# New places for the steps of an attention head within its period of 40 ticks, and per-column places for the split of the next weights

## The chip, the cores and the metric

The kernel runs on one core of a Trainium2 chip. The metric is the device time of one execution in microseconds (us). The engines that compute are TensorE (PE, matmuls), VectorE (DVE), ScalarE (ACT) and GpSimd (POOL); SyncE (SP) issues most of the DMAs. Each engine works through its own list of instructions strictly in order, and waits for the others by semaphores.

## The reference

One streaming inference step of one layer: 512 frames of a new stream (the prompt) and 64 frames of a running stream (the sample, which has 512 cached keys and values), 2048 channels each, in float32.

```python
def stick_breaking(q, k, v, q_pos, k_pos):
    z = jnp.einsum('bqhd,bkhd->bhqk', q, k) / math.sqrt(HEAD_DIM)
    mask = (k_pos[None, :] < q_pos[:, None])[None, None]
    log_1mb = jnp.where(mask, jax.nn.log_sigmoid(-z), 0.0)
    after = lax.cumsum(log_1mb, axis=3, reverse=True) - log_1mb
    w = jnp.where(mask, jnp.exp(jax.nn.log_sigmoid(z) + after), 0.0)
    return jnp.einsum('bhqk,bkhd->bqhd', w, v)

def hybrid_layer(x, ...):
    hn = rmsnorm(x, g_norm1)
    q, k, v, gb, gc, hc = split(hn @ w_in)       # 3 x 8 heads x 128, 3 x 1024 channels
    q = rmsnorm(q, g_q); k = rmsnorm(k, g_k)     # per head
    o_attn = stick_breaking_blocks(q, k, v, P)   # per head, causal; sample against cache and itself
    o_conv = gb * conv3(gc * hc)
    x = x + concat(rmsnorm(o_attn), rmsnorm(o_conv)) @ w_out
    h2 = rmsnorm(x, g_norm2)
    return x + (silu(h2 @ w_gate) * (h2 @ w_up)) @ w_down, k, v, new_conv
```

Keys and values of the new frames are outputs too.

## The kernel before

Frames lie along the free axis (576 = 512 + 64, in two halves of 288), channels on the 128 partitions. A float32 product is made of three matmuls on parts rounded to a shorter format: high x high, low x high, high x low. So each weight block is split into a high part (`whi`, a cast on ACT) and a low part (`wlo`, a subtraction on DVE), and so is everything else that is multiplied.

The kernel runs in stages: the input and the first four columns of 128 outputs of `w_in` (EARLY); units of a fast matrix scheme for other columns; then the stage of this document, from about 184 us on: ten columns of `w_in` (LATE: q and k of heads 4 to 7, v of heads 6 and 7), and after them six columns of the first convolution groups, while the eight attention heads are computed between their matmuls; then the convolution, the output projection and the feed-forward part, to the end at 2356 us.

In the stage of the heads `project` makes one column: `next_weight` hands over the split weights, then `product` runs over 16 blocks of 128 channels for each half of the frames, three matmuls a block (`step`, line 246). After each block comes `pipe.tick()`. A `Pipeline` holds generators with due times counted in these ticks; at a tick it runs those that are due, and what they emit goes to the end of each engine's list. A column is 32 ticks. So the ticks count places in the program: PE's order, and through `manual_schedule` that of ACT, DVE, POOL and SP too, is written out by hand in this stage, and a step's number says behind which matmuls and which other steps its instructions stand. It does not say when they run. In a tick, the generator that was put back first goes first.

Head h is the generator `attend(h)`, spawned at tick 1 + 40 h (`PERIOD`). It sorts the steps of `head_steps(h)` by their numbers, 0 to 127, and emits them. Three heads are under way at a time: while head h does its steps 0 to 39, head h - 1 does 40 to 79 and head h - 2 does 80 to 119. For the last head the numbers over 72 are squeezed to three quarters. In the order of the data, the steps of a head are:

- `load` (SP) brings q and k as 576 tokens; `square` (ACT) and `sums` (DVE) make their sums; `small` (PE, DVE, ACT), `root` (DVE) the scales; `norm` and `turn` (DVE) scale and transpose; `high` (ACT: `qh`, `qe`, `kh`, `ke`) and `low` (DVE) split them. `weigh` (POOL) and `keys` (SP, eight stores) put the new keys out. For heads 0 and 1, DVE also transposes in `square`.
- `cached` (SP) and `turn_cached` (DVE) bring the cached keys; `sample` (PE, then `zc` copied by ACT) makes the scores of the sample.
- For the prompt there are three groups of keys, b = 2 (which holds the blocks 2 and 3), 1 and 0, each with its PSUM bank `z2`, `z1`, `z0`: `score` (PE, then three activations), `add` (DVE, then the mask on POOL), `cast` (ACT), `rest` (DVE, then for b = 2 and 1 a sum on POOL), `sum_high` (ACT) and `sum_low` (DVE) of the sums, `run` (PE, DVE, an exponential and a cast on ACT), `run_low` (DVE).
- `values` (SP), `store` (SP), `v_high` (ACT: `vh`), `v_low` (DVE: `vl`); `out` and `outs` (PE) multiply values into the PSUM tile `po`; `copy` (ACT, line 1024) takes `po` out into `o_attn`, whose tiles are `o_oa` and `o_ob`.
- For the sample: `soft` (ACT), `soft_add` (DVE, five operations on POOL), `sp_high` (ACT: `sph`), `sp_low` (DVE), `sample_sums` (PE into the PSUM tile `cz`, line 1031, then DVE), `weights` (ACT), `load_cv` (SP), `sample_out` (PE `os`, ACT).
- `squares` (ACT, then POOL adds into `acc_a`), at the end of a head. Squares and the sums of `square` share one scratch area.

The PSUM tag `misc` has two buffers, taken in turn by `ss` (`small`), `zs` (`sample`), `po`, `cz` and `os`; in the order of emission `cz` takes the buffer that `po` had. Tiles of `t1` have one buffer each, apart from `vtok` with two.

Beside the heads, each LATE column i spawns `split_later(i, end)`: at its tick 7 both halves of the next weights' high part on ACT, at 9 and 11 their low parts on DVE, at 16 the load of the weights after the next on SP into the one raw buffer. When a half is done, `late_evac` transposes it out of PSUM (DVE `El`) and POOL issues its store to `qk_dram`.

```python
    def split_later(i, end):
        yield 7
        if i + 1 < end:
            yield from split_parts()
        yield 5
        if i >= len(EARLY) and i + 2 < end:
            load_weight()
```

Of the kernel before, what the change touches and what calls it, by code (L numbers as in the profile page):

```python
# [24 lines left out]
NH = 8  # L25
# [17 lines left out]
LATE = [(0, 4), (1, 4), (0, 5), (1, 5), (0, 6), (1, 6), (0, 7), (1, 7), (2, 6), (2, 7)]  # L43
PERIOD = 40


# [52 lines left out]
def tile_hybrid_stream_step(  # L99
# [100 lines left out]
    def split_parts():  # L200
# [567 lines left out]
    def head_steps(h):  # L768
# [31 lines left out]
        for i, n in enumerate("qk"):  # L800

            @at((0, 5)[i])
            def _(i=i, n=n):
                E[n] = t1.tile([P, T], F32, tag="E" + n, name="E" + n)
                nc.sync.dma_start(out=E[n], in_=qk_dram[2 * h + i])

            @at((12, 20)[i])
            def _(i=i, n=n):
                if (i, h) in EARLY:
                    nc.vector.transpose(out=E[n], in_=E[n])  # L810
                nc.scalar.activation(out=sq, in_=E[n], func=AF.Square)

            @at((14, 22)[i])
# [3 lines left out]
        @at(28)  # L817
# [6 lines left out]
        @at(31)  # L824
# [8 lines left out]
        @at(33)  # L833
        def _():
            stt(out=t_, in0=y, scalar=-0.5, in1=y, op0=ALU.mult, op1=ALU.mult)
            nc.vector.tensor_tensor(out=t_, in0=t_, in1=ms, op=ALU.mult)
            stt(out=ms, in0=t_, scalar=1.5, in1=y, op0=ALU.add, op1=ALU.mult)

        for i, n in enumerate("qk"):
            gain = (gqs, col("gk"))[i]  # L840

            @at((33, 35)[i])
            def _(i=i, n=n):
                r = ms[:, NB * i : NB * (i + 1)].unsqueeze(2).to_broadcast([P, NB, 32])
                nc.vector.tensor_tensor(out=chunks(E[n]), in0=chunks(E[n]), in1=r, op=ALU.mult)

            @at((35, 36)[i])
            def _(n=n):
                nc.vector.transpose(out=new(n + "f", T), in_=E[n])

            @at((37, 39)[i])
            def _(n=n, gain=gain):
                f = w[n + "f"]
                nc.scalar.activation(out=new(n + "h", cut[n], F32R), in_=f[:, : cut[n]], func=AF.Copy, scale=gain)
                nc.scalar.activation(out=new(n + "e", T - 3 * P), in_=f[:, 3 * P :], func=AF.Copy, scale=gain)

            @at((39, 41)[i])
            def _(n=n, gain=gain):
                stt(out=new(n + "l", TP, F32R)[:, : cut[n]] if n == "q" else new(n + "l", cut[n], F32R),
                    in0=w[n + "f"][:, : cut[n]], scalar=gain, in1=w[n + "h"].bitcast(F32), op0=ALU.mult,  # L860
                    op1=ALU.subtract)

        @at(42)
# [4 lines left out]
        @at(46)  # L868
# [4 lines left out]
        @at(47)  # L873
        def _():
            nc.vector.transpose(out=w["cK"], in_=w["cK"])
# [8 lines left out]

        for b, t in ((2, 52), (1, 56), (0, 61)):
# [9 lines left out]
        for b, t in ((2, 56), (1, 59), (0, 67)):  # L895

            @at(t)
# [5 lines left out]
        for b, t in ((2, 58), (1, 63), (0, 71)):  # L903

            @at(t)
            def _(b=b):
                cast(new(f"ph{b}", full[b], F32R), w[f"pr{b}"])

        for b, t in ((2, 60), (1, 65), (0, 75)):

            @at(t)
            def _(b=b):
                low(new(f"pl{b}", full[b], F32R), w[f"pr{b}"], w[f"ph{b}"])
                if b:
                    nc.gpsimd.tensor_tensor(out=pb(b)[:, P:], in0=pb(b)[:, P:], in1=pb(b + 1), op=ALU.add)

        for b, t0, t1_ in ((1, 65, 67), (0, 69, 71)):

            @at(t0)
            def _(b=b):  # L920
                cast(new(f"s{b}h", full[b + 1] if b == 0 else 256, F32R), pb(b + 1))

            @at(t1_)
# [3 lines left out]
        @at(62)  # L927
# [7 lines left out]
        @at(66)  # L935
        def _():
            load_values(h)

        @at(80)
        def _():  # L940
            soft_log(sp[:, :320], zc)

        @at(82)
# [8 lines left out]
        @at(72)  # L952
# [5 lines left out]
        @at(83)  # L958
        def _():
# [13 lines left out]

        for b, t in ((2, 78), (1, 81), (0, 86)):

            @at(t)
            def _(b=b):
# [5 lines left out]

        for b, t in ((2, 82), (1, 85), (0, 90)):

            @at(t)
# [4 lines left out]
        @at(83)  # L991
# [4 lines left out]
        @at(84)  # L996
# [4 lines left out]
        @at(90)  # L1001
        def _():
            w["po"] = misc("po")
            mm(w["po"][:, 384:512], w["vtok"][:, 3, :], pb(3), start=True, stop=False, skip_group_check=True)

        for i, t in ((2, 95), (1, 98), (0, 101)):

            @at(t)
            def _(i=i):
# [3 lines left out]

        @at(92)
        def _():
            cast(new("sph", T, F32R), sp)

        @at(94)
        def _():
            low(new("spl", T, F32R), sp, w["sph"])  # L1020

        @at(102)
        def _():
# [3 lines left out]

        @at(108)
        def _():
# [7 lines left out]

        @at(110)
        def _():
            nc.scalar.activation(out=w["ws"][:, TS:], in_=w["ws"][:, TS:], func=AF.Exp)  # L1040

        @at(118)
        def _():
# [6 lines left out]
        for i, (a, b) in enumerate(HALVES):  # L1050

            @at((119 if h == NH - 1 else 125) + 2 * i)
            def _(i=i, a=a, b=b):
# [1291 lines left out]
```

## Time and profile before

| what | us |
|---|---|
| median of 3 runs (lowest, highest) | 2358.49 (2356.91, 2360.97) |
| the profiled execution's own time | 2358.04 |
| its span, first to last instruction | 2356.3 |
| busy in the span: PE / DVE / ACT / POOL | 2326.7 / 1916.2 / 1164.5 / 280.3 |
| PE busy in the 20 us from 240, 340, 380 | 16.87, 16.10, 15.85 |
| PE busy in the 20 us from 440 and 460 | 20.00, 20.00 |

The profile is one execution. A group's row gives busy time and mean duration; a row of the waits tells which engine stood idle, before which instruction, until which other instruction ended, in total, how often, and the longest. In a timeline the bracket at the end of a row is the idle time before it and what ended it. Names such as `cz L1031` are tile and line of the kernel. PE's times are those of pipelined matmuls, which overlap: durations of neighbours must not be added, distances of their starts may be.

### The profile page before, as it was taken

Reading aid. Unit: us, or ns where it says so; the run is one execution under the profiler, and the core shown is the slowest. Engines: PE = TensorE matmul, PEld = TensorE weight load, DVE = VectorE, ACT = ScalarE, POOL = GpSimd, SP = SyncE. Lnnn points to the kernel's source line nnn. Section 1 sums busy time; section 2 is a strip of 40 time slices with the busy share of each in tenths; the row PEclk is TensorE's granted clock in tenths of the full one; section 3 lists DMA queues with packets and bytes.
Section 4 is the critical chain, followed back from the end, with each engine's and each line's share of the span. In section 5 each row is a group of like instructions: output and inputs, shape, how many; then the busy total and the mean of one; then the engine's idle time right before and its main releaser. Section 6 shows DMA issues by size and latency. Waiting matters only on the chain.

```text
span 2356.3 us, 43717 instructions
## 1 busy us (share of the span) xinstructions
PE 2326.7 (99%) x17437; PEld 2315.5 (98%) x17437; DVE 1916.2 (81%) x2846; ACT 1164.5 (49%) x2021; POOL 280.3 (12%) x394
## 2 busy tenths in 40 slices
PE   9999988999999999999999999999999999999999
PEld 9999888999999999999999999999999999999999
DVE  7976767688887889888888888888888777887886
ACT  7534766544445555444444444444444444444444
POOL 1002333121111220000000000000000001431121
PEclk9999999999999999999999999999999999999999
DMA  8775454784368645444444444444444945885643
GB/s 274 206 208 160 121 138 107 232 284 124 110 227 233 190 159 159 141 153 137 138 153 128 147 151 130 147 146 134 149 141 140 342 137 191 234 234 187 206 130 104
DMA packets 584869, 402.54 MB, mean 171 GB/s; under 512 B 91870, under 2 KB 571864, under 8 KB 584664
## 3 DMA queue, kind: packets, MB, share of 16 engines
q1 hardware_dynamic: 574136, 378.56, 51.5%
q0 software_dynamic: 10160, 20.94, 3.9%
q8 instruction: 136, 2.23, 0.4%
q14 instruction: 69, 0.57, 0.1%
q10 hardware_dynamic: 368, 0.24, 0.0%
HBM read 303.53 MB, written 96.16 MB: 170 GB/s over the span
## 4 chain that ended last, share of the span: by engine, by line
PE 87%; DVE 4%; ACT 3%; DMA 2%; issue 1%; POOL 1%; SPq 0%; DVEq 0%; ACTq 0%; POOLq 0%
PE psy L1991 35%; PE psw L1991 18%; PE psx L1991 9%; PE psy L1478 6%; PE pjo L246 4%; PE pj L246 4%; PE psw L1478 3%; PE psy L1125 3%; PE psx L1478 2%; PE psw L1125 1%; PE psx L1125 1%; ACT whi L205 1%; DVE wlo L208 0%; DMA vtok<-vt_dram 0%; DMA form_dram<-hf 0%
## 5 line engine op out<-in xcount | busy, mean ns | idle before, releaser
L1991 PE MATMUL psy<-h_s,whl 128*128 128x288 f32 x2787 | 411.4, 294 | 0.0
L1991 PEld LDWEIGHTS psy<-h_s,whl 128*128 128x128 f32 x2787 | 383.6, 188 | 0.0
L256 DVE TENSOR_TENSOR whl<-raw_a,whl 128x1024 fp32r<-128x1024 f32 (+4 forms) x296 | 319.2, 1080 | 57.3 <-ACT whl L255 56.4
L1991 PE MATMUL psw<-t,whl 128*128 128x288 f32 x2400 | 347.5, 295 | 0.0
L1991 PEld LDWEIGHTS psw<-t,whl 128*128 128x128 f32 x2400 | 327.6, 188 | 0.3 <-DVE whl L256 0.2
L255 ACT CAST whl<-raw_a 128x1024 fp32r<-128x1024 f32 (+4 forms) x296 | 268.1, 906 | 102.1 <-issue 35.3
L246 PE MATMUL pj<-x,whi 128*128 128x288 f32 x1248 | 275.4, 302 | 0.3 <-DVE x L409 0.3
L256 DVE TENSOR_TENSOR whl<-raw_b,whl 128x1024 fp32r<-128x1024 f32 (+5 forms) x190 | 199.3, 1049 | 66.2 <-ACT whl L255 65.2
L255 ACT CAST whl<-raw_b 128x1024 fp32r<-128x1024 f32 (+5 forms) x190 | 165.4, 871 | 166.1 <-issue 73.2
L2001 ACT COPY part<-psy 128x288 f32<-128x288 f32 x242 | 96.4, 398 | 282.6 <-PE psy L1991 281.4
L246 PEld LDWEIGHTS pj<-x,whi 128*128 128x128 f32 x1248 | 210.3, 191 | 1.1 <-DVE x L409 0.6
L246 PE MATMUL pj<-x,wlo 128*128 128x288 f32 x624 | 186.1, 298 | 0.1
L1991 PE MATMUL psy<-t2t,whl 128*128 128x288 f32 x1212 | 183.4, 295 | 0.0
L1991 PE MATMUL psy<-b22m,whl 128*128 128x288 f32 x1212 | 183.0, 294 | 0.0
L1991 PE MATMUL psx<-h_s,whl 128*128 128x288 f32 x1185 | 173.7, 295 | 0.0
L1991 PEld LDWEIGHTS psy<-t2t,whl 128*128 128x128 f32 x1212 | 168.4, 188 | 0.2 <-DVE whl L256 0.2
L1991 PEld LDWEIGHTS psy<-b22m,whl 128*128 128x128 f32 x1212 | 168.2, 188 | 0.0
L1991 PEld LDWEIGHTS psx<-h_s,whl 128*128 128x128 f32 x1185 | 162.7, 188 | 0.0
L255 ACT CAST whl<-s 128x1024 fp32r<-128x1024 f32 (+5 forms) x81 | 72.3, 893 | 101.3 <-PE psw L1991 101.3
L246 PEld LDWEIGHTS pj<-x,wlo 128*128 128x128 f32 x624 | 119.2, 191 | 0.7 <-DVE wlo L494 0.3
L1770 POOL DMA_DIRECT2D hid_dram<-form x3 | 2.3, 752 | 971.5 <-DVE form L256 970.2
L1991 PE MATMUL psy<-t,whl 128*128 128x288 f32 x576 | 106.7, 295 | 0.0
(533 smaller groups left out, 4546.6 us busy)
## 6 DMA issues: line engine op xcount, KB each, us to landing
hid_dram<-form SPq DMA_DIRECT2D x147, 288.0 KB, 2.2
raw_a<-in_w_in_dram SPq DMA_DIRECT2D x31, 1024.0 KB, 5.4
raw_a<-in_w_gate_dram SPq DMA_DIRECT2D x22, 1024.0 KB, 5.5
raw_a<-in_w_up_dram SPq DMA_DIRECT2D x22, 1024.0 KB, 5.7
raw_b<-in_w_gate_dram SPq DMA_DIRECT2D x22, 1024.0 KB, 6.8
raw_b<-in_w_up_dram SPq DMA_DIRECT2D x22, 1024.0 KB, 6.5
h_s<-hid_dram SPq DMA_DIRECT2D x10, 2016.0 KB, 11.8
raw_a<-in_w_out_dram SPq DMA_DIRECT2D x16, 1024.0 KB, 5.5
```

The source lines that it names most:

```text
L205: nc.scalar.copy(out=hi[:, a : a + 1024], in_=raw[:, a : a + 1024])
L246: mm(ps, w_[:, k, csl], x_, start=(k == 0 and n == 0), stop=(k == nk - 1 and n == 2))
L255: nc.scalar.copy(out=hi, in_=src)
L256: (lo_eng or nc.vector).tensor_tensor(out=lo, in0=src, in1=hi.bitcast(F32), op=ALU.subtract)
L1125: mm(ps, whl[:, w_, j, :], x_, start=(start and j == 0 and q == 0), stop=(j == NP - 1 and q == 2), skip_group_check=True)
L1478: mm(ps, whl[:, w_, j, :], x_, start=(start and j == 0 and q == 0), stop=(j == m - 1 and q == 2), skip_group_check=True)
L1770: q.dma_start(out=hid_dram[fp][2 * n - 2 : 2 * n].rearrange("f p t -> p f t"), in_=t.bitcast(F32))
L1991: mm(ps, whl[:, w_, j, :], x_, start=(start and j == 0 and q == 0), stop=(j == len(xs_) - 1 and q == 2), skip_group_check=True)
L2001: nc.scalar.copy(out=t, in_=st["y"])
```

## The change

Every number of a step moves into a table `STEP`; many get another value. For the ten LATE columns `split_later` hands over to a new function, `split_at`, which places the two casts, the two subtractions and the load by a table `WEIGHT` with one row of five ticks a column, the halves one by one. The instructions are the same; what changes is the order in which they are emitted on each engine. Tuples of `STEP` are for (q, k), for b = (0, 1, 2), or for the two halves.

| step | before | after | step | before | after |
|---|---|---|---|---|---|
| load q, k | 0, 5 | 0, 11 | values | 66 | 62 |
| square | 12, 20 | 13, 19 | store | 72 | 74 |
| sums | 14, 22 | 17, 21 | soft, soft_add | 80, 82 | 78, 83 |
| small, root | 31, 33 | 27, 30 | load_cv | 83 | 80 |
| norm q, k | 33, 35 | 35, 33 | run 0, 1, 2 | 86, 81, 78 | 86, 81, 72 |
| low q, k | 39, 41 | 40, 41 | run_low 0, 1, 2 | 90, 85, 82 | 89, 87, 86 |
| keys | 46 | 47 | v_high, v_low | 83, 84 | 75, 83 |
| score 0, 1, 2 | 61, 56, 52 | 61, 56, 50 | out | 90 | 87 |
| add 0, 1, 2 | 67, 59, 56 | 63, 62, 55 | outs 0, 1, 2 | 101, 98, 95 | 101, 97, 95 |
| cast 0, 1, 2 | 71, 63, 58 | 69, 63, 58 | sp_high, sp_low | 92, 94 | 92, 100 |
| rest 0, 1, 2 | 75, 65, 60 | 77, 65, 62 | sample_sums, weights | 108, 110 | 104, 109 |
| sum_high 0, 1 | 69, 65 | 67, 65 | sample_out | 118 | 116 |
| sum_low 0, 1 | 71, 67 | 77, 67 | squares | 125, 127 | 124, 125 |
| sample | 62 | 59 | squares, last head | 119, 121 | 119, 121 |

`cached` (28), `turn` (35, 36), `high` (37, 39), `weigh` (42), `turn_cached` (47) and `copy` (102) keep theirs.

```diff
+STEP = dict(
+    load=(0, 11), square=(13, 19), sums=(17, 21), cached=28, small=27, root=30, norm=(35, 33), turn=(35, 36),
...
+WEIGHT = [
+    (9, 11, 9, 14, 18), (11, 16, 11, 14, 24), (10, 12, 10, 17, 20), (7, 9, 7, 12, 12), (6, 11, 7, 10, 21), (6,
+    10, 7, 11, 19), (6, 9, 7, 11, 19), (7, 10, 7, 11, 16), (9, 11, 9, 17, 18), (5, 8, 6, 11, 16)]
...
+    def split_at(i, end):
+        w = {}
+
+        def begin():
+            w["raw"], w["two"] = raws[i + 1], weight_split(i + 1)
+
+        def high(a):
+            nc.scalar.copy(out=w["two"][0][:, a : a + 1024], in_=w["raw"][:, a : a + 1024])
+
+        def rest(a):
+            nc.vector.tensor_tensor(out=w["two"][1][:, a : a + 1024], in0=w["raw"][:, a : a + 1024],
+                                    in1=w["two"][0][:, a : a + 1024].bitcast(F32), op=ALU.subtract)
+
+        h0, l0, h1, l1, again = WEIGHT[i - len(EARLY)]
+        now = 0
+        steps = [(h0, begin), (h0, lambda: high(0)), (h1, lambda: high(1024)), (l0, lambda: rest(0)),
+                 (l1, lambda: rest(1024))] + [(again, load_weight)] * (i + 2 < end)
+        for t, work in sorted(steps, key=lambda step: step[0]):
+            if t > now:
+                yield t - now
+                now = t
+            work()
+
     def split_later(i, end):
+        if len(EARLY) <= i < len(EARLY) + len(LATE):
+            yield from split_at(i, end)
+            return
         yield 7
...
-            @at((0, 5)[i])
+            @at(STEP["load"][i])
...
-        for b, t in ((2, 78), (1, 81), (0, 86)):
-
-            @at(t)
+        for b in (2, 1, 0):
+
+            @at(STEP["run"][b])
...
-        @at(108)
+        @at(STEP["sample_sums"])
```

More of the change, by code (lines that the diff above doesn't have):

```diff
@@ L44 @@
 PERIOD = 40
+STEP = dict(
+    load=(0, 11), square=(13, 19), sums=(17, 21), cached=28, small=27, root=30, norm=(35, 33), turn=(35, 36),
+    high=(37, 39), low=(40, 41), weigh=42, keys=47, turn_cached=47, score=(61, 56, 50), add=(63, 62, 55),
+    cast=(69, 63, 58), rest=(77, 65, 62), sum_high=(67, 65), sum_low=(77, 67), sample=59, values=62, store=74,
+    soft=78, soft_add=83, load_cv=80, run=(86, 81, 72), run_low=(89, 87, 86), v_high=75, v_low=83, out=87,
+    outs=(101, 97, 95), sp_high=92, sp_low=100, copy=102, sample_sums=104, weights=109, sample_out=116,
+    squares=(124, 125), last=(119, 121))
+WEIGHT = [
+    (9, 11, 9, 14, 18), (11, 16, 11, 14, 24), (10, 12, 10, 17, 20), (7, 9, 7, 12, 12), (6, 11, 7, 10, 21), (6,
+    10, 7, 11, 19), (6, 9, 7, 11, 19), (7, 10, 7, 11, 16), (9, 11, 9, 17, 18), (5, 8, 6, 11, 16)]
 DOWN = (
@@ L805, in _ @@
                 nc.sync.dma_start(out=E[n], in_=qk_dram[2 * h + i])
-            @at((12, 20)[i])
+            @at(STEP["square"][i])
             def _(i=i, n=n):
@@ L822, in _ @@
                                   in_=ck[:, h, 32 * q : 32 * (q + 1)].rearrange("(b t) c -> t b c", t=32))
-        @at(31)
+        @at(STEP["small"])
         def _():
@@ L831, in _ @@
             nc.scalar.activation(out=y, in_=y, func=AF.Exp, scale=-0.5)
-        @at(33)
+        @at(STEP["root"])
         def _():
@@ L840, in head_steps @@
             gain = (gqs, col("gk"))[i]
-            @at((33, 35)[i])
+            @at(STEP["norm"][i])
             def _(i=i, n=n):
@@ L866, in _ @@
                                     in1=gk_t.unsqueeze(1).to_broadcast([P, NB, 32]), op=ALU.mult)
-        @at(46)
+        @at(STEP["keys"])
         def _():
@@ L883, in scores @@
                 mm(zb(i), w[a_][:, kk], w[b_][:, q0:TP], start=(n == 0), stop=False, skip_group_check=True)
-        for b, t in ((2, 52), (1, 56), (0, 61)):
-            @at(t)
+        for b in (2, 1, 0):
+            @at(STEP["score"][b])
             def _(b=b):
@@ L893, in _ @@
                 soft_log(new(f"pr{b}", full[b]), w[f"z{b}"][:, : full[b]])
-        for b, t in ((2, 56), (1, 59), (0, 67)):
-            @at(t)
+        for b in (2, 1, 0):
+            @at(STEP["add"][b])
             def _(b=b):
@@ L901, in _ @@
                     later_queries(pb(i)[:, :P], -1)
-        for b, t in ((2, 58), (1, 63), (0, 71)):
-            @at(t)
+        for b in (2, 1, 0):
+            @at(STEP["cast"][b])
             def _(b=b):
                 cast(new(f"ph{b}", full[b], F32R), w[f"pr{b}"])
-        for b, t in ((2, 60), (1, 65), (0, 75)):
-            @at(t)
+        for b in (2, 1, 0):
+            @at(STEP["rest"][b])
             def _(b=b):
@@ L933, in _ @@
             nc.scalar.copy(out=zc, in_=zs[:, TS : TS + 320])
-        @at(66)
+        @at(STEP["values"])
         def _():
             load_values(h)
-        @at(80)
+        @at(STEP["soft"])
         def _():
             soft_log(sp[:, :320], zc)
-        @at(82)
+        @at(STEP["soft_add"])
         def _():
@@ L950, in _ @@
                                         in1=sp[:, (b + 1) * TS : (b + 2) * TS], op=ALU.add)
-        @at(72)
+        @at(STEP["store"])
         def _():
@@ L956, in _ @@
             nc.sync.dma_start(out=vs[:, h, :], in_=vtok[TS:, 4, :])
-        @at(83)
+        @at(STEP["load_cv"])
         def _():
@@ L982, in _ @@
                 cast(w[f"ph{b}"][:, : pb(b).shape[1]], pb(b))
-        for b, t in ((2, 82), (1, 85), (0, 90)):
-            @at(t)
+        for b in (2, 1, 0):
+            @at(STEP["run_low"][b])
             def _(b=b):
@@ L994, in _ @@
             cast(w["vh"], w["vtok"][:, 0:3, :])
-        @at(84)
+        @at(STEP["v_low"])
         def _():
@@ L999, in _ @@
             low(w["vl"], w["vtok"][:, 0:3, :], w["vh"])
-        @at(90)
+        @at(STEP["out"])
         def _():
@@ L1012, in _ @@
                        stop=(i == 0 and n == 2), **kw)
-        @at(92)
+        @at(STEP["sp_high"])
         def _():
             cast(new("sph", T, F32R), sp)
-        @at(94)
+        @at(STEP["sp_low"])
         def _():
             low(new("spl", T, F32R), sp, w["sph"])
-        @at(102)
+        @at(STEP["copy"])
         def _():
@@ L1050, in head_steps @@
         for i, (a, b) in enumerate(HALVES):
-            @at((119 if h == NH - 1 else 125) + 2 * i)
+            @at(STEP["last" if h == NH - 1 else "squares"][i])
             def _(i=i, a=a, b=b):
```

34 lines of the change are left out of this document (17 added, 17 removed).

## The prediction

> **What bounds the kernel now.** I read the page first, for the engine that fills the span.
>
> ```profile
> span 2356.3 us, 43717 instructions
> PE 2326.7 (99%) x17437; PEld 2315.5 (98%) x17437; DVE 1916.2 (81%) x2846; ACT 1164.5 (49%) x2021; POOL 280.3 (12%) x394
> ```
>
> TensorE (PE) is busy for all but 29.6 us, so an edit that leaves the matmuls alone can win only PE's idle time and what a slow clock costs. Next the waits of PE from 184 to 444 us, the stretch with the head steps.
>
> ```profile
> PE cz L1031 <- ACT o_oa L1024: 8.8, 4, 2.5
> PE cz L1031 <- ACT o_ob L1024: 7.7, 3, 4.1
> PE os L1047 <- issue: 1.7, 2, 1.5
> PE po L1011 <- DVE vl L750: 1.2, 3, 0.7
> PE po L1004 <- ACT pr L981: 1.0, 1, 1.0
> PE po L1011 <- ACT vh L747: 0.9, 2, 0.5
> PE z L883 <- DVE kl L859: 0.2, 1, 0.2
> ```
>
> The sum is 21.5 us, 16.5 of it in one place, once a head: the first matmul of `sample_sums` waits for ScalarE (ACT) to copy `po` out (step `copy`), because both share a PSUM buffer. The windows that follow run from one such matmul to the next, and then over the 3.4 us behind the three longest stalls; columns are length, PE, PEld, DVE, ACT, POOL busy, granted clock, DMA.
>
> ```profile
> 271.49:300.15 28.66, 26.35 (x180) 25.78 (x181) 19.86 (x37) 19.78 (x42) 8.99 (x17) 0.94 0.64 163
> 300.15:328.32 28.17, 25.06 (x180) 24.27 (x180) 19.84 (x38) 19.67 (x42) 10.06 (x18) 1.00 0.48 125
> 357.78:388.50 30.72, 26.39 (x181) 25.63 (x181) 23.22 (x43) 21.55 (x44) 10.48 (x15) 0.94 0.47 114
> 271.50:275.00 3.50, 3.50 (x16) 3.50 (x17) 2.47 (x7) 1.86 (x5) 1.16 (x2) 0.57 1.15 293
> 357.30:360.70 3.40, 2.92 (x12) 2.92 (x13) 1.54 (x2) 3.36 (x6) 0.00 (x0) 0.51 0.00 0
> 388.10:391.50 3.40, 3.00 (x12) 3.00 (x13) 2.25 (x5) 1.90 (x5) 1.17 (x2) 0.50 1.15 296
> ```
>
> A head's period takes 28 to 31 us though PE has 25.06 us of work in it at full clock. No engine is full: VectorE (DVE) and ACT have about 20 of 28. Behind three stalls the clock was halved, which costs 3.5 x 0.43 + 3.4 x 0.49 + 3.4 x 0.50 = 4.9 us. So at stake is 21.5 + 4.9 = 26.4 us, 1.1% of the time.
>
> ```profile
> 271.49 0.41 PE L1031 MATMUL cz<-sph,trir 128*128 128x320 f32 x1 [2.46 <-ACT o_oa L1024]
> 328.32 0.42 PE L1031 MATMUL cz<-sph,trir 128*128 128x320 f32 x1 [2.36 <-ACT o_oa L1024]
> 388.50 0.64 PE L1031 MATMUL cz<-sph,trir 128*128 128x320 f32 x1 [4.15 <-ACT o_ob L1024]
> ```
>
> A stall of 2.36 us kept the full clock; stalls of 2.46 us and more lost it. [...]
>
> Why is the copy late? ACT in one period, the rows that wait and the end:
>
> ```profile
> 273.69 0.52 ACT L747 CAST s0h<-pr 128x384 fp32r<-128x384 f32 x1 [1.20 <-POOL pr L915]
> 278.42 0.72 ACT L854 ACTIVATE qh<-qf,gqs 128x512 fp32r<-128x512 f32 x1 [2.30 <-DVE qf L849]
> 280.48 0.49 ACT L981 ACTIVATE pr<-z 128x384 f32<-128x384 f32 x1 [0.89 <-DVE z L980]
> 286.41 0.60 ACT L981 ACTIVATE pr<-z 128x512 f32<-128x512 f32 x1 [1.09 <-DVE z L980]
> 287.56 1.99 ACT L205 CAST whi<-raw_a 128x1024 fp32r<-128x1024 f32 x2
> 291.16 0.69 ACT L811 ACTIVATE raw_a<-Eq 128x576 f32<-128x576 f32 x1 [1.26 <-POOL acc_a L599]
> 296.72 0.51 ACT L747 CAST ph<-pr 128x384 fp32r<-128x384 f32 x1 [1.31 <-POOL pr L729]
> 297.14 0.68 ACT L811 ACTIVATE raw_a<-Ek 128x576 f32<-128x576 f32 x1
> 297.73 0.57 ACT L753 ACTIVATE pr<-z 128x512 f32<-128x512 f32 x1
> 299.53 0.57 ACT L1024 COPY o_oa<-po 128x512 f32<-128x512 f32 x1
> ```
>
> None of these waits is for PE. ACT, DVE and GpSimd (POOL) wait for one another in a ring that is 28 us long, every engine in its written order; PE runs ahead and stops at the one matmul that needs the ring's end. The order sets the period.
>
> **The change, part by part.** No instruction is added or removed; every engine gets another order. "Tick t" is a step's place modulo 40.
>
> *Two waits for POOL go.* `cast2` (296.72) waits for POOL's mask, which waits for DVE's `add2`, which stands behind `sp_low`. Now `add2` is at tick 15, ahead of `sp_low` at 20, and the three activations of `score1` stand between it and `cast2`: 1.31 us goes. `square_q` (291.16) writes the scratch that POOL reads for `squares1`; before, `squares1` came after run0 and, here, behind the weight cast of 1.99 us. Now it comes at tick 5, ahead of `run0`, and `score2` and `sp_high` lie before `square_q`: 1.26 us goes.
>
> *The wait of run0 goes.* DVE had `run_low2`, `v_low` and `run_low1` before it. Both `run_low` now stand behind run0's own DVE work, and `vh` is cast half a period earlier, so that `v_low` need not wait: 1.09 us goes.
>
> *run2 moves ahead of norm* (tick 38 to 32). Queued behind its DVE work, which waits for PE, are `norm_k`, `norm_q`, both turns, and behind those ACT's `qh`; PE's next scores wait for these. On the way to `qh` come the two DVE operations of run2 and one more norm, while `rest0` leaves it.
>
> ```profile
> L980 DVE SCALAR_TENSOR_TENSOR z<-z,acA 128x128 f32<-128x128 f32 x4 | 1.2, 293 | 0.0
> L845 DVE TENSOR_TENSOR Ek<-Ek,raw_a 128x576 f32<-128x576 f32 x1 | 0.7, 717 | 0.0
> L750 DVE TENSOR_TENSOR pl<-pr,ph 128x512 fp32r<-128x512 f32 x2 | 1.4, 684 | 0.0
> ```
>
> That is 2 x 0.29 + 0.72 - 0.68 = 0.6, plus a wait for PE that I put at 1.0 (run2's matmuls come five ticks behind `small`, 2.0 us, which ACT and DVE spend on the root for half of it): 1.6 us later. In return ACT does run2's 0.49 and its cast (256 columns, 0.3 by the 0.51 of 384 at 296.72) in the hole of 2.30 us before `qh`, and loses the wait of 0.89 and the `vh` cast (384 columns, 0.51) behind it: 2.2 us. Net 0.6 us gained; from 0.9 lost (a PE wait of 2.5) to 1.6 gained (none).
>
> *The ring then* is 28.66 - 1.31 - 1.26 - 1.09 - 0.6 = 24.4 us, under PE's 25.06: PE becomes the bound.
>
> *The copy moves closer to its reader.* `sample_sums` goes from tick 28 to 24, `copy` stays at 22, and `score0` now stands before `outs0` on PE.
>
> ```profile
> 184.43 12.69 PE pj L246 x96
> 292.38 0.40 PE L1011 MATMUL po<-ph,vh 128*128 128x512 f32 x1
> 293.08 0.39 PE L883 MATMUL z<-qh,kh 128*128 128x512 f32 x1
> 430.65 0.29 PE L246 MATMUL pj<-x,whi 128*128 128x288 f32 x1
> 430.85 0.59 ACT L1024 COPY o_ob<-po 128x512 f32<-128x512 f32 x1 [0.70 <-PE po L1011]
> ```
>
> A tick is 12.69 / 32 = 0.40 us, `outs0` 0.70. From the end of `score0` PE needs 0.70 + 3 x 0.40 = 1.90 us to `sample_sums`. ACT starts 0.20 after PE has issued (430.65 to 430.85), needs 299.53 - 297.73 = 1.80 for the three activations and 0.57 for the copy, and 0.05 to the matmul: 2.62. So even an idle ACT leaves 0.7 us a head; the four ticks given up (1.6 us) were cover that is gone. For seven heads (the last has no score behind it) that is 5.0 us, all below the stalls that lost clock.
>
> *The weight columns.* The casts move by -2 to +4 ticks (0.8 us back to 1.6 us on), the reload by up to 8; next weights are first needed at tick 32 of a column, at least 14 ticks behind the last part. Most periods hold one pair of casts (1.99 us, in the 24.4 above). Two hold two pairs (ACT 21.55 in 357.78:388.50), before and after: 24.4 + 2.0 = 26.4, which is 1.3 over PE, say 1.0 each because part falls into ACT's remaining waits: 2 us, from 0 to 4. The transposes and low parts on DVE stay inside its slack (20 of 25 us).
>
> *The small waits* (os, po, z: 5.0 us) come from the same lateness; `vh` is earlier by eight ticks, and I keep 1 us of the 5.0.
>
> *DMA orders.* The load of k goes from tick 5 to 11, and past the eight stores of `keys`, which stay in front.
>
> ```profile
> 283.69 0.33 SPq L805 DMA_DIRECT2D Ek<-qk_dram  x1
> 284.07 4.26 SPq L735 DMA_DIRECT2D out_dram<-qf  x8
> DMA to landing us min/median/max: 2.9/3.0/4.7
> ```
>
> Both wait for the same POOL product, so the load is issued 4.3 us later and lands 7.3 us behind that product (9.0 with the longest landing). The square of k came 297.14 - 283.69 = 13.4 us behind it and is now earlier by the 2.6 us of the two POOL waits and at most 1: about 10. Hidden by 1 to 2.7 us; nothing. `values`, `store`, `load_cv` move by 4 ticks or less.
>
> **Sum**: left over 5.0 + 2 + 1 = 8.0 us, gained 26.4 - 8.0 = 18.4. Against the profiled execution's own 2358.04 us (span 2356.3 and 1.7 around it) that is 2339.6; it lies 0.45 under the median of 2358.49, so 2340.
>
> **Rivals.** *The ring stays ahead of PE.* If run2's wait takes the 2.5 us and run0's stays, the ring is 24.4 + 1.5 + 1.1 = 27.0; PE waits 1.9 a head, no clock is lost: 7 x 1.9 + 2.5 for the rest = 15.8 left, 10.6 gained, 2348. For it speaks that DVE is the queue all chains pass; against it that two removed waits rest on order alone. *The stall only moves*: a wait refills what another gave back, as the four lost ticks (1.6 us) do at once; if only the POOL waits go (2.6) and run2 gives 1 back, nothing remains: 2358. Against it: PE's wait ends with ACT's ring, and no other row of ACT waits for PE. *Slower: the load of k.* It stands behind the eight stores; landing late it stops ACT at the square of k, with `zc`, `score0` and `copy` behind. It decides from a landing of about 7 us after issue (the 10 us, and 1.2 that ACT would then idle before `score0` anyway, less 4.3): at 9 us it adds 2.1 to the 0.7, over 2.46 in all, so each head loses 2.8 and 1.7 of clock: 7 x 4.5 + 3 for the rest = 34.5 against 26.4, 2367. [...]
>
> **Numbers.** The forecast (2340) 0.60, the ring ahead (2348) 0.20, only moved (2358) 0.10, slower (2367) 0.10. The range reaches from almost no residue (1.5 us left, 2333) past the second case, to 2352, with 0.8 inside. A measurement of this kernel can tell about 0.2%, 4.7 us: faster 0.80, same 0.10, slower 0.10.
>
> **What would show it.** Right: the wait of cz for `o_oa` and `o_ob` falls from 16.5 to 4 to 9 us, no window at half clock between 200 and 420 us, periods of 25.5 to 26.5 us; ACT's waits for POOL at `ph` and before the square of q are gone, that of `qh` shrinks; the wait of run2 on DVE for PE appears, near 1 us. Wrong: a wait of ACT on the load of k, stalls of cz over 2.4 us, or a new PE wait at the scores (`kl` late) or `run0` (`s0l`, now at tick 37, late).

## The result and the profile after

The kernel after takes 2332.3 us (median of 4 runs, 2329.9 to 2335.1) where the kernel before, on the same chip, takes 2358.9 (2356.9 to 2361.0): ratio 0.9888, 95% interval 0.9870 to 0.9905. The forecast was 2340 with a range from 2333 to 2352: the direction was right, the gain came out larger, and the time lies 0.7 us below the range. The profiled execution of after took 2329.9 us with a span of 2327.9, against 2358.0 and 2356.3 before. The first two rows of its page:

```profile
span 2327.9 us, 43743 instructions
PE 2317.2 (100%) x17437; PEld 2309.0 (99%) x17437; DVE 1916.5 (82%) x2846; ACT 1162.8 (50%) x2021; POOL 286.0 (12%) x394
```

The busy time of DVE, ACT and POOL stands where it stood; PE's idle time fell from 29.6 us to 10.7. The waits of PE from 184 to 444 us after the change (engine, tile and line, whom it waited for, us in total, times, longest):

```profile
PE z L919 <- DVE kl L895: 1.3, 1, 1.3
PE os L1083 <- issue: 0.2, 1, 0.2
```

21.5 us have become 1.5, and the wait of `cz` isn't there at all. The matmul `cz` once a head, and two periods from one to the next (length, PE, PEld, DVE, ACT, POOL busy, granted clock, DMA), the second with two pairs of weight casts on ACT:

```profile
L1067 PE MATMUL cz<-sph,trir x8: 306/306/309, 237.5 to 403.3; 128*128 128x320 f32 x8
...
287.19:311.68 24.49, 24.49 (x183) 24.15 (x181) 19.51 (x37) 19.67 (x42) 10.42 (x18) 1.00 0.59 148
336.17:360.65 24.48, 24.48 (x182) 24.14 (x181) 22.44 (x41) 21.01 (x44) 9.02 (x15) 1.00 0.50 122
```

PE has no hole in either, and the granted clock is 1.00. ACT in one head, with the idle time in brackets, and two rows of PE:

```profile
270.25 0.73 ACT L890 ACTIVATE qh<-qf,gqs 128x512 fp32r<-128x512 f32 x1
...
281.87 0.69 ACT L847 ACTIVATE raw_a<-Eq 128x576 f32<-128x576 f32 x1 [1.53 <-POOL acc_a L635]
...
283.95 0.50 ACT L783 CAST ph<-pr 128x384 fp32r<-128x384 f32 x1
...
284.94 0.41 ACT L969 COPY raw_a<-zs 128x320 f32<-128x320 f32 x1
285.51 0.60 ACT L789 ACTIVATE pr<-z 128x512 f32<-128x512 f32 x1 [0.16 <-PE z L919]
...
287.34 0.57 ACT L1060 COPY o_oa<-po 128x512 f32<-128x512 f32 x1
```

```profile
285.77 0.39 PE L1047 MATMUL po<-pl,vh 128*128 128x512 f32 x1
287.19 0.31 PE L1067 MATMUL cz<-sph,trir 128*128 128x320 f32 x1
```

The waits before `qh` and before `ph` (POOL's mask) are gone here; that before the square of q isn't. ACT now waits for PE's score at 285.51. And `cz` starts at 287.19, 0.15 us before ACT begins the copy of `po` that it used to wait for.

Over all heads, ACT's waits of these kinds from 220 to 400 us, before and then after (in the last row, DVE's operations of run2 wait for PE):

```profile
ACT qh L854 <- DVE qf L849: 18.8, 7, 3.4
...
ACT ph L747 <- POOL pr L729: 5.2, 6, 1.3
ACT raw_a L811 <- POOL acc_a L599: 4.5, 4, 1.3
```

```profile
ACT qh L890 <- DVE qf L885: 3.5, 4, 2.1
ACT raw_a L847 <- POOL acc_a L635: 2.7, 3, 1.5
ACT raw_a L847 <- DMA Ek<-qk_dram: 2.4, 2, 1.7
...
ACT ph L783 <- POOL pr L765: 1.1, 1, 1.1
...
DVE z L1016 <- PE z L1003: 1.7, 3, 0.7
```

### The profile page after: what moved, and what is told of

It reads as the page before. It is cut to its first block, busy times and chain, and to the rows that moved or that the text cites. A ratio compares the mean times of both kernels' runs of the same rounds, so it can differ in the third digit from the quotient of the medians.

```text
span 2327.9 us, 43743 instructions
## 1 busy us (share of the span) xinstructions
PE 2317.2 (100%) x17437; PEld 2309.0 (99%) x17437; DVE 1916.5 (82%) x2846; ACT 1162.8 (50%) x2021; POOL 286.0 (12%) x394
## 4 chain that ended last, share of the span: by engine, by line
PE 91%; DMA 3%; DVE 3%; SPq 2%; issue 1%; ACT 0%; ACTq 0%; DVEq 0%
PE psy L2027 34%; PE psw L2027 17%; PE psx L2027 9%; PE pj L282 7%; PE psy L1514 6%; PE pjo L282 4%; PE psw L1514 3%; PE psy L1161 3%; PE psx L1514 2%; PE psw L1161 1%; DMA raw_a<-in_w_in_dram 1%; PE psx L1161 1%; DMA form_dram<-hf 1%; SPq L2224 1%; DMA raw_b<-in_w_down_dram 1%
```

## The experiments

Each time is a median, beside the kernel before on the same chip. The line above each edit in a diff names the run and the kernel that it starts from; of the long lines of `STEP` only the entries that change are shown.

**Why cz no longer waits.** In the program as built, a new tile takes the `misc` buffer whose last reader was emitted first. Before, `copy` (the last reader of `po`) is emitted ahead of `zc`, the copy of `zs` at the end of `sample`, and `cz` gets `po`'s buffer. After, `sample` is three ticks earlier, `zc` comes first, and `cz` gets the buffer of `zs`. Four runs move this. Two move one copy alone: `copy` a tick later on the kernel before, `zc` later on the kernel after. Two move the whole of `sample`, its matmuls too: earlier on the kernel before, later on the kernel after.

```diff
 e1_copy103 (before): copy
-        @at(102)
+        @at(103)
 e8_sample59 (before): sample
-        @at(62)
+        @at(59)
 e2_sample63 (after)
-    sample=59
+    sample=63
 e5_zc_late (after)
-    sample=59
+    sample=59, zc=63
...
-            nc.scalar.copy(out=zc, in_=zs[:, TS : TS + 320])
+            w["zs"] = zs
+
+        @at(STEP["zc"])
+        def _():
+            nc.scalar.copy(out=zc, in_=w["zs"][:, TS : TS + 320])
```

> The kernel before with one number changed: copy from 102 to 103, one tick later. Theory B (the buffer): cz gets the misc buffer that is given back first in the written order. Before, the copy of po stands ahead of zc, so cz waits for po; with copy at 103, zc stands ahead, cz takes the buffer of zs and the next ss, three ticks behind cz, takes the one of po. The stall moves from cz to ss and shrinks by the 1.9 us that PE needs for cz (0.66) and three ticks (1.2), and stays under 2.4 us, so the half clock goes too: 7 x 1.9 + 5 = 18 us, 2341. Theory R (the ring of my prediction, with a fixed exposure behind the copy): a copy one tick later cannot help, 2358 to 2362.

> The kernel before with one number changed: sample from 62 to 59, so that zc stands ahead of the scores of b = 0 on ACT and cz takes the buffer of zs. Theory Z (most of the gain is that cz no longer stands behind the three activations of score0 and the copy, 2.4 us): cz waits about 0.5 us or not at all, ss waits for the copy, about 1 us; no half clock; 16 us gained, 2342. Theory R (the ring of ACT, DVE and POOL has to be shortened by the other steps): stalls of 2 us and more stay at ss, 2352 to 2358.

> The changed kernel with sample at 63 in place of 59, so that zc stands behind the copy and cz takes the buffer of po again. Theory B with the prediction's own term for the copy (0.7 us a head, seven heads): 5 us more than the changed kernel's 2332, 2337, with cz waiting 0.5 to 0.9 us for o_oa or o_ob. If the ring itself is what the change mended and the buffer does not matter: 2332. If the buffer is most of the gain: 2345 and more.

> The changed kernel with the copy of zc alone put off: the matmuls of sample stay at 59, ACT copies zc at 63, behind the copy of po, so that cz takes the buffer of po. Theory F (my term for the copy): PE reaches cz 1.90 us behind the scores of b = 0, ACT's copy ends 2.62 us behind them; cz waits 0.5 to 0.9 us in each of seven heads, 5 us in all, plus 3 us in periods with two pairs of casts: 2337 to 2341. Rival, that the copy's place is harmless: 2332 to 2333.

The waits of PE from 184 to 444 us in the kernel before with the copy a tick later:

```profile
PE cz L1031 <- ACT raw_a L933: 14.5, 6, 3.2
```

Line 933 is `zc`: the buffer did change hands, and `cz` waits nearly as long (14.5 us for 16.5) for `zc`, which now stands on ACT where the copy of `po` stood. 2361.1 against 2358.1 (ratio 1.0011, 1.0002 to 1.0020). With `sample` at 59 alone it is 2358.95 against 2359.04 (1.0000, 0.9991 to 1.0009): the stall is spread over `os` (6.1 us), `cz` (5.1), `ss` and `po`. As long as ACT's work arrives every 28 us it doesn't matter for which piece PE waits.

On the kernel after it does matter. `sample` at 63 gives 2333.95 (0.9897, 0.9884 to 0.9911), less than the 2337 expected, with 3.2 us of waits at `cz` in three heads: this edit also puts the matmuls of `sample` on PE between `po` and `cz`, about 1 us of work in which ACT can copy:

```profile
260.91 0.38 PE L968 MATMUL zs<-qe,ke 128*128 128x128 f32 x2
261.13 1.06 PE L968 MATMUL zs<-qe,cK 128*128 128x128 f32 x8
...
262.64 0.41 PE L1067 MATMUL cz<-sph,trir 128*128 128x320 f32 x1
```

`zc` late, which leaves PE's order alone, gives 2337.7 (0.9910, 0.9894 to 0.9925), and there the waits and four of the matmuls of `cz` read:

```profile
PE cz L1071 <- ACT o_oa L1064: 3.3, 4, 1.4
PE cz L1071 <- ACT o_ob L1064: 2.3, 3, 1.1
```

```profile
264.10 0.41 PE L1071 MATMUL cz<-sph,trir 128*128 128x320 f32 x1 [0.61 <-ACT o_oa L1064]
...
289.52 0.41 PE L1071 MATMUL cz<-sph,trir 128*128 128x320 f32 x1 [0.61 <-ACT o_oa L1064]
...
340.81 0.41 PE L1071 MATMUL cz<-sph,trir 128*128 128x320 f32 x1 [1.06 <-ACT o_ob L1064]
...
366.23 0.41 PE L1071 MATMUL cz<-sph,trir 128*128 128x320 f32 x1 [0.61 <-ACT o_ob L1064]
```

That is the 0.7 us a head of the prediction: 0.61 by the rows, in five of the seven heads that wait. From start to start the period is 25.42 (264.10 to 289.52) instead of 24.48, so the shared buffer costs 0.94 a head. The period from 340.81 to 366.23, in which ACT has two pairs of weight casts (at 341.39, 358.77 and 360.30), is 25.42 long too. The two longer waits, 1.06 at 340.81 and 1.4 in the first head, have another cause: just ahead of them ACT stood idle for the load of k, and the copy came later.

```profile
235.70 0.69 ACT L847 ACTIVATE raw_a<-Ek 128x576 f32<-128x576 f32 x1 [1.81 <-DMA Ek<-qk_dram]
...
337.79 0.69 ACT L847 ACTIVATE raw_a<-Ek 128x576 f32<-128x576 f32 x1 [0.92 <-DMA Ek<-qk_dram]
```

**The weight columns.** One run has the kernel after with the columns as before, one the kernel before with the new columns.

```diff
 e3_old_columns (after), in split_later
-        if len(EARLY) <= i < len(EARLY) + len(LATE):
-            yield from split_at(i, end)
-            return
 e4_columns_only (before), with WEIGHT and split_at as in the change
+        if len(EARLY) <= i < len(EARLY) + len(LATE):
+            yield from split_at(i, end)
+            return
```

> The changed kernel with the columns of before (casts at 7, low parts at 9 and 11, load at 16). Prediction's term: the columns' moves lie inside the slack, 2332 to 2334. Rival, that the columns' ticks are needed for the gain: some heads stall by 1 to 2 us, 2336 to 2345.

> The kernel before with only the columns' table of the change. Prediction's term: nothing, 2358 within 3 us, stalls of cz as before. Rival, that the columns alone free ACT ahead of the copy: 2 to 4 heads gain 1 to 2 us and the half clock behind them, 2348 to 2353.

On the kernel before they change nothing: 2357.1 against 2358.1 (0.9996, 0.9987 to 1.0005). Without them the kernel after takes 2337.4 (0.9914, 0.9901 to 0.9928), 5 us more. Its longest wait of PE in the stage:

```profile
PE ss L860 <- DVE raw_a L848: 2.5, 1, 2.5
```

PE waits for DVE's sums, with a half clock behind it at 216.6 us (0.50 over 3.4 us, which is 1.7 us). `os` waits another 1.3. So the 5 us are mostly one event in one head. The columns pay only where PE has become the bound.

**Giving single parts of the change back.** Each of these is the kernel after with some steps at their old places.

```diff
 e7_pool_waits (after)
-    sp_low=100, squares=(124, 125)
+    sp_low=94, squares=(125, 127)
 e6_run2_back (after)
-    run=(86, 81, 72), v_high=75
+    run=(86, 81, 78), v_high=83
 e11_scores_back (after)
-    score=(61, 56, 50), add=(63, 62, 55), cast=(69, 63, 58), rest=(77, 65, 62), sum_high=(67, 65), sum_low=(77, 67)
+    score=(61, 56, 52), add=(67, 59, 56), cast=(71, 63, 58), rest=(75, 65, 60), sum_high=(69, 65), sum_low=(71, 67)
 e16_all_but_load (after)
-    load=(0, 11), keys=47
+    load=(0, 5), keys=46
 e9_small_back (after); e10_small_only (before) is the same edit the other way
-    small=27, root=30, sample_sums=104, weights=109, sample_out=116
+    small=31, root=33, sample_sums=108, weights=110, sample_out=118
```

> The changed kernel with sp_low back at 94 (ahead of add2 again) and squares back at 125, 127. Prediction's term: ACT waits for POOL's mask (1.3 us) and for acc_a (1.3 us) again in each head; the ring grows by 2.6 to 27.0 and PE waits 1.9 us a head, 13 us more, 2345. Theory Z: the slack that the early zc gives (2.4 us at cz, 1.9 at ss) takes it: 2332 to 2335.

> The changed kernel with run2 back at 78 and v_high back at 83. Prediction's term: the ring grows by 0.6 us a head, to 25.0, no more than PE's work: 2332 to 2335, and ACT's wait of 2.3 us at qh is back. Rival, that this move carries the gain (norm waits less, or run2 and vh fill the hole): stalls at cz or po of 1 us and more a head, 2339 and more.

> The changed kernel with score, add, cast, rest, sum_high and sum_low as before. Theory S: most of the gain stays, 2332 to 2337. If instead add0 and the masks, which now stand earlier on DVE and POOL, shorten the ring: ACT's wait for POOL at the sum cast (2 us a head) is back, 2338 to 2350.

> The kernel after with the loads at 0 and 5 and keys at 46 as before: the load of k is issued ahead of the eight stores of keys again. Theory L (the later load is hidden, as the prediction says): 2331 to 2334, no new wait, and the 2.4 us that ACT waits for Ek in the kernel after go. Rival (the stores ahead of the load are worth something, because the load at 11 takes k into a free stretch): over 2335, with a wait of keys' stores or of cached behind it.

> The changed kernel with the group of sample_sums, weights, small, root and sample_out back at 108, 110, 31, 33, 118. Theory S (the group's move by four ticks shortens the ring of ACT, DVE and POOL, since small then stands ahead of the sum cast that waits for POOL and of weights): ACT's wait at qh is 2 us a head again, the ring is 2 us longer, PE stalls 1 to 2 us a head, 2338 to 2346. Theory P (the prediction's attribution: waits for POOL, run0 and run2, without this group): 2332 to 2334.

The first four cost nothing: 2332.0 (ratio 0.9889), 2332.7 (0.9894), 2331.3 (0.9886), 2330.4 (0.9881, 0.9867 to 0.9894). None can be told from the kernel after, so none is a version that beats it. But they do not all cost nothing for the same reason. With `sp_low` and `squares` at their old places the waits that were to return did not: ACT waits 0.9 us for POOL's mask and 1.7 for `acc_a` (1.1 and 2.7 in the kernel after), so in this order other steps keep these waits away. With run2 back the wait before `qh` grows by 2 us in all, to 5.5, and PE does not feel it. A run that takes one part away from the finished kernel says little on what that part had brought. The last one costs 5 us (2337.3, 0.9912): ACT's waits for `qf` before `qh` come back (12.6 us from 220 to 400, for 3.5), PE waits 3.0 us for `pl`, and the clock drops behind one of these waits (0.62 from 330.2 to 333.6). The same group alone on the kernel before:

> The kernel before with only that group moved, to 104, 109, 27, 30, 116; cz keeps the buffer of po. Theory S: qh waits 0 to 1 us in place of 2.3 to 3.4, the ring is some 26, PE stalls about 1 us a head and keeps its clock, 2338 to 2346. Theory P: 2356 to 2360, stalls as before.

2361.4 against 2358.5 (1.0013, 1.0004 to 1.0022). PE's waits from 184 to 444:

```profile
PE cz L1031 <- ACT o_oa L1024: 13.4, 4, 3.9
PE cz L1031 <- ACT o_ob L1024: 8.0, 3, 3.7
```

16.5 us at `cz` became 21.4: the four ticks of cover between `copy` and `sample_sums` were lost, as the prediction said of them, while ACT's wait before `qh` fell from 18.8 us to 3.2 and came back elsewhere (ACT's waits at `small` 13.2, at `os` 16.3).

**The value steps.** They are `soft`, `soft_add`, `run`, `run_low`, `v_high`, `v_low`, `out`, `outs`, `sp_low` and `squares`, in which the prediction had put most of what leaves the ring. First they were given back.

```diff
 e12_values_back (after)
-    soft=78, soft_add=83, run=(86, 81, 72), run_low=(89, 87, 86), v_high=75, v_low=83, out=87,
-    outs=(101, 97, 95), sp_low=100, squares=(124, 125)
+    soft=80, soft_add=82, run=(86, 81, 78), run_low=(90, 85, 82), v_high=83, v_low=84, out=90,
+    outs=(101, 98, 95), sp_low=94, squares=(125, 127)
 e13_values_back_83 (e12_values_back)
-    soft=80, soft_add=82
+    soft=78, soft_add=83
```

> The changed kernel with soft, soft_add, run, run_low, v_high, v_low, out, outs, sp_low and squares as before: all of the parts to which the prediction gave its 2.96 us a head (the waits for POOL 2.57 less what add keeps, run0 1.09, run2 0.6). Theory P: ring 27 and more, 2345 to 2358. Theory S: 2332 to 2337.

> The kernel after with the value steps (soft, run, run_low, v_high, v_low, out, outs, sp_low, squares) at their old places as in the run before it, but soft_add kept at 83, behind weigh on GpSimd, so that the load of k is not late. Theory K (the run before lost its 20 us to the late load of k): ACT's wait for Ek falls from 12.7 to under 3 us and the time is 2332 to 2337. Theory V (the order of the value steps themselves carries the gain, as the prediction's wait of run0 and net of run2 say): Ek waits are gone too, but ACT's pr<-z waits stay near 17 us, cz waits 5 to 12 us, and the time is 2343 to 2352.

The first took 2352.4 us (0.9977, 0.9967 to 0.9987): 20 us of the gain lost. Waits of PE (184 to 444 us), ACT and POOL (220 to 400):

```profile
PE cz L1067 <- ACT raw_a L969: 14.1, 6, 3.5
...
ACT raw_a L847 <- DMA Ek<-qk_dram: 12.7, 6, 4.0
...
POOL raw_a L982 <- DVE raw_a L794: 44.2, 7, 12.2
```

But this run mixes two things. In its order POOL does `soft_add` (line 982), which waits long for DVE, ahead of `weigh`; the stores of `keys` wait for `weigh`, and the load of k stands behind them on SP. It is the prediction's slower rival at work, set off by POOL's order: ACT stands 2.1 us a head at the square of k. The second run moves `soft` and `soft_add` back to 78 and 83, so that `weigh` is first again. The time is 2335.7 (0.9901, 0.9886 to 0.9916), and ACT's wait and POOL's:

```profile
ACT raw_a L842 <- DMA Ek<-qk_dram: 0.4, 1, 0.4
...
POOL raw_a L977 <- DVE raw_a L789: 10.1, 7, 2.7
```

So 16.6 of the 20 us went with the change of `soft` and `soft_add` by two ticks and one, together with the wait for k; the old order of the other value steps costs 3.4, hardly more than the noise (2333.8 to 2336.5 against 2329.9 to 2335.1). The theory that their order carries the gain of the finished kernel fell (it wanted 2343 or more). Whether it is because they do little, or because the other steps leave them room, was tried from the other side.

```diff
 e14_values_only (before): the edit of e12_values_back the other way, and
-    values=66, store=72, load_cv=83
+    values=62, store=74, load_cv=80
 e15_values_small (e14_values_only)
-    small=31, root=33, sample_sums=108, weights=110, sample_out=118
+    small=27, root=30, sample_sums=104, weights=109, sample_out=116
 e18_splow_only (before)
-    sp_low=94
+    sp_low=100
 e19_run_only (before)
-    run=(86, 81, 78), run_low=(90, 85, 82), v_high=83, v_low=84
+    run=(86, 81, 72), run_low=(89, 87, 86), v_high=75, v_low=83
```

> The kernel before, with only the value steps (soft, soft_add, run, run_low, v_high, v_low, out, outs, sp_low, squares, values, store, load_cv) at their new places. Theory V: they shorten the ring by the waits of run0, run2 and both for GpSimd, 3 to 4 us a head, so cz waits fall below 9 us and the time is 2338 to 2346. Theory C (no part suffices, the whole order has to fit): 2355 to 2361, with cz still waiting 15 us or more.

> The run before this one with small, root, sample_sums, weights and sample_out at their new places as well (root and the norms come earlier by 3 to 4 ticks). Theory V+S (the two groups together are the gain: norms early, values late behind them): 2334 to 2342, qh's wait of ACT under 5 us. Theory C: 2352 to 2361, with the wait of cz for the copy, which now has four ticks less cover, at 15 us or more.

> The kernel before with sp_low alone moved (tick 14 to 20). Theory R (the waits on the ring add up, as the prediction's sum has it): the wait of ph for GpSimd's mask, 5.2 us in 220 to 400 us, falls below 1 us, the ring is about 1 us a head shorter, the stalls of cz shrink from 16 to 8 to 11 us, two or three half clocks go: 2345 to 2351. Theory M (one wait alone only moves; the chain takes another way through DVE): ph's wait goes, but ACT's other waits grow by as much: 2355 to 2360.

> The kernel before with run, run_low, v_high and v_low alone at their new places (run2 ahead of norm, both run_low behind run0's DVE work). Theory R: by the prediction's sum this takes 1.09 and 0.6 us a head from the ring: qh's wait of ACT falls from 18.8 to under 9, cz's stalls fall below 9 us, 2341 to 2347. Theory M: the waits move to s0h, square or the mask: 2354 to 2360.

| kernel before, with | time, us | gain, us | ratio (95%) | first to eighth cz, us |
|---|---|---|---|---|
| nothing | 2357.9 | | | 190.5 |
| sp_low alone | 2350.5 | 7.3 | 0.9969 (0.9956 to 0.9981) | 185.7 |
| run, run_low, v_high, v_low | 2346.8 | 11.1 | 0.9950 (0.9937 to 0.9964) | 181.4 |
| all value steps | 2339.6 | 18.2 | 0.9920 (0.9907 to 0.9934) | 176.6 |
| value steps and small | 2342.1 | 15.6 | 0.9932 (0.9920 to 0.9945) | |
| all but most value steps (e13) | 2335.7 | 22.1 | 0.9901 (0.9886 to 0.9916) | 170.5 |

The rows of `cz` (first and last start of eight) for the kernel before, with `sp_low`, with `run`, and with all value steps, one fence each:

```profile
L1031 PE MATMUL cz<-sph,trir x8: 305/412/635, 242.5 to 433.0; 128*128 128x320 f32 x8
```

```profile
L1059 PE MATMUL cz<-sph,trir x8: 305/414/417, 240.6 to 426.3; 128*128 128x320 f32 x8
```

```profile
L1059 PE MATMUL cz<-sph,trir x8: 305/413/637, 240.0 to 421.4; 128*128 128x320 f32 x8
```

```profile
L1059 PE MATMUL cz<-sph,trir x8: 309/412/415, 238.2 to 414.8; 128*128 128x320 f32 x8
```

4.8 us and 9.1 us shorter, and 13.9 together: the terms add up, as the prediction's sum took them to, and the gains do (7.3 + 11.1 = 18.4 against 18.2). The agreement is closer than the parts bear out. Summed over windows of 3.4 us from 184 to 446, the lowered clock costs 5.1 us in the kernel before, 5.1 in each of the two runs with one part, and 1.7 with all value steps: 3.4 of the 18.2 us are clock that neither part gives back alone. ACT's waits show which go. With `sp_low` alone POOL's mask is no longer among the waits and `qh` stands untouched; with the run steps `qh` falls from 18.8 us to 10.5 and the mask (`ph`) stays, each from 220 to 400 us:

```profile
ACT qh L882 <- DVE qf L877: 18.8, 7, 3.4
...
ACT s0h L775 <- POOL pr L943: 8.9, 6, 2.1
```

```profile
ACT qh L882 <- DVE qf L877: 10.5, 7, 2.2
...
ACT ph L775 <- POOL pr L757: 6.3, 7, 1.3
```

With all value steps `cz` still waits 6.9 us for the copy; with `small` beside them 9.7, and that run missed its 2334 to 2342 by a little: once more the lost cover without the buffer that makes up for it.

## Why the prediction was right or wrong

**The ring sets the period, and the order sets the ring: right.** Two edits of the order alone, with not an instruction changed, take 7.3 and 11.1 us. The mask wait was put at 1.31 us a head, 9.2 over seven; the two run terms at 1.09 + 0.6 = 1.69, 11.8 over seven. Measured 7.3 and 11.1: the first came out a fifth smaller, the second close. Part of that is luck. Between the first and the eighth `cz` the runs are 4.8 and 9.1 us shorter, 0.7 and 1.3 us a head, about half and three quarters of the terms; the rest lies ahead of the first `cz` (240.6 and 240.0 for 242.5). The wait of run2's DVE work for PE, put near 1 us a head, comes three times from 220 to 400 us in the kernel after, 1.7 us in all.

**"PE becomes the bound": right, but the sum that led there, 28.66 to 24.4, is not confirmed.** Once PE is the bound, the length of the ring no longer shows. "1.26 us goes" at the square of q did not hold: from 220 to 400 us ACT still waits 2.7 us there (4.5 before), and 8.8 in the kernel with only the value steps. The two edits that were to take POOL's waits away did not bring them back when they were undone in the kernel after; by the prediction's terms that run was to take 2345 and took 2332.0. And `small` with its group, to which the prediction gave no gain, costs 5 us when it is undone there. The kernel after without most value steps still gains 22.1 us, from what the prediction gave no value (`small`, `sample`, the scores, squares of q and k, the columns) and from `soft`, `soft_add`, `values`, `store` and `load_cv`. The two halves overlap, 22.1 + 18.2 against 26.6. PE is a floor under both, and these last five steps are in both; the two causes were not separated. What in the first half shortens the ring was not taken apart further; single pieces of it on the kernel before gave nothing (`sample`, `small`, columns).

**"The copy moves closer to its reader", 5.0 us left over: this step failed.** Its arithmetic was right for the shared buffer (0.7 a head against 0.61 in the rows of the run with `zc` late; 5.0 us in all against the 5.4 between 2337.7 and 2332.3), but its premise, that `cz` and `po` share one also after the change, was not: `cz` waits nowhere, where 4 to 9 us were forecast, and the period is 24.48 us, where 25.5 to 26.5 were. The text ahead of the prediction said that the buffers are taken in turn; what decides is which last reader is emitted first, and the move of `sample` by three ticks, which the prediction did not cost, turns it. Neither part works alone: the buffer gives nothing while the ring is slow, and the fast ring leaves 5 us while the buffer is shared (1.7 us where the matmuls of `sample` cover the copy).

**"Two hold two pairs: 2 us": this term failed too, and not because of the buffer.** The window 336.17:360.65 has ACT at 21.0 us and still takes 24.48. With the buffer shared, in the run with `zc` late, the period with two pairs takes 25.42 like the others. So the ring took up the second pair, where the prediction's ring of 24.4 + 2.0 could not. Why it had that room was not tried.

**The stake of 26.4 us: too small by 2 to 3.** By the medians 26.6 us were gained and 1.5 us of waits are left, so 28.1 were to be had; by the profiled times (2358.0 - 2329.9 = 28.1 gained, the profiled execution of after being the fastest of its four) 29.6. The bracketed idle time runs from the modelled end of the matmul before, and that is later than the time at which its successor starts when nothing stalls (in the kernel after, matmuls of 0.29 us start 0.13 apart at 199.83 and 199.96). So PE's busy time in a stalled period, 25.06 us, held more than its work: a period without a hole has 24.48 with about as many matmuls. The run with `zc` late shows the same: 0.61 in brackets, 0.94 in the period.

The account by medians: forecast 18.4 gained, measured 26.6, 8.2 more. 8.0 - 1.5 = 6.5 of it is residue that did not come, the other 1.7 the stake. With 1.5 left, the prediction's own sum gives 2358.5 - 26.4 + 1.5 = 2333.6, the lower end of its range: the residue took the time to that edge, the stake past it.

**The new places of the columns, given nothing of their own: too little.** They save 5 us against the old ones once PE is the bound, and nothing on the kernel before.

**The small waits kept at 1 us: about right**, 1.5, in another place (`kl` once, which the prediction had named as a possible new wait).

**The rivals.** The ring ahead of PE, and only moved stalls, did not come. The slower one, the load of k, has its trace in the kernel after: ACT waits 2.4 us in all for `Ek`, in two places, where the prediction had it hidden. It costs nothing that can be measured there (without it 2330.4, inside the spread); where `cz` shares the buffer it shows as 1.4 and 1.06 us in place of 0.61; and it is a part of the 16.6 us in the run where POOL's order makes it later.

## What to carry to other kernels

Where several engines wait for one another in a fixed order, sum the waits around the ring and compare them with the work of the fullest engine; here the terms that left the ring added up about as summed until that engine was the bound, and beyond this point taking a part away mostly showed nothing. Follow also which buffer a tile will get: a step moved past another one's last read can change whom a matmul waits for. Measure a part by adding it to the kernel before as well as by taking it out of the kernel after, and look, on each engine, at which of two steps due at the same tick comes first (here `weigh` and `soft_add` on POOL).

## What was not expected of the hardware

**The length of a stall does not decide on the clock.** Before, a stall of 2.36 us kept the full clock (1.00 from 328.40 to 331.80 us) and one of 2.46 lost it (0.57 from 271.50 to 275.00), and the prediction took that for a bound. In the run with `sp_low` alone a stall of 1.78 us is followed by a clock of 0.60 (the matmul, then a window of 3.4 us from it):

```profile
323.99 0.41 PE L1059 MATMUL cz<-sph,trir 128*128 128x320 f32 x1 [1.78 <-ACT o_oa L1052]
```

```profile
324.00:327.40 3.40, 3.40 (x17) 3.40 (x18) 2.54 (x7) 1.76 (x5) 1.68 (x3) 0.60 0.15 47
```

In the run with the value steps given back, one of 2.81 us is not (the matmul, then the 3.4 us from it, at 1.00):

```profile
267.97 0.41 PE L1067 MATMUL cz<-sph,trir 128*128 128x320 f32 x1 [2.81 <-ACT raw_a L969]
```

```profile
268.00:271.40 3.40, 3.12 (x22) 2.89 (x23) 2.90 (x7) 2.87 (x6) 1.38 (x4) 1.00 0.99 243
```

So something beside the length of a stall counts; what it is, no run of this case shows.
